# Pairing the scan's k/q loads and the two directions' decay loads in a bidirectional gated DeltaNet layer with windowed attention

## The chip, the cores and the metric

One NeuronCore of one Trainium2 chip runs the whole layer. The metric is the device time of one execution, in microseconds (us). Where a profile is read, one execution of the same program was taken by the hardware profiler; its time and its span are given beside the median of the unprofiled runs.

## What is computed

The layer takes x (2048 tokens of width 1024), normalises it, projects it once, and feeds two head groups: a gated DeltaNet with 4 heads of width 128 that is scanned forward and backward, and windowed attention with 8 query heads. Their outputs are concatenated, projected and added to x. Only the DeltaNet's part bears on the change. For each head and direction, with g the running sum of the log decays inside a chunk:

```python
decay = jnp.exp(jnp.where(incl, g[..., :, None] - g[..., None, :], -jnp.inf))
m = jnp.where(strict, jnp.einsum('bhncd,bhnsd->bhncs', k_beta, k) * decay, 0.0)
a_intra = jnp.where(incl, jnp.einsum('bhncd,bhnsd->bhncs', q, k) * decay, 0.0)
...
def step(state, inp):
    q_i, k_i, u_i, w_i, g_i, a_i = inp
    v_new = u_i - jnp.einsum('bhcd,bhde->bhce', w_i, state)
    o = (jnp.einsum('bhcd,bhde->bhce', q_i * jnp.exp(g_i)[..., None], state)
         + jnp.einsum('bhcs,bhse->bhce', a_i, v_new))
...
    state = state * jnp.exp(g_last)[..., None, None] + jnp.einsum('bhcd,bhce->bhde', k_dec, v_new)
```

All arithmetic is in 32-bit floats. The kernel uses chunks of 128 tokens, so a head has 16 chunks (NCH = 16) and each direction takes 16 dependent steps.

## The kernel before, in words

**Phase A** (`phase_a`) projects x, convolves, and writes intermediates to scratch tensors in device memory (DRAM): k and q of head h transposed into `kq_d[h]` (128 feature rows, a plane for k and one for q, 2048 token columns), v into `v_d[h]`, and the gates. It computes the windowed attention too. In its second half it calls `delta_setup` (L431), which forms the running decay sums and writes them as a small table `gr_d` (L496 to L502): for each direction d, 64 rows of 128 values, row c*4+h for chunk c and head h. The sums of one head over four neighbouring chunks therefore lie in four pieces of 128 values (512 bytes) that are 2 KB apart. For head 0 only (NDEC = 1) `delta_setup` also computes the full decay matrices ahead of time: for each group of four chunks and each direction it loads the table's pieces broadcast to 128 partitions (L512), adds the mask on GpSimd (L513), takes exponentials on ScalarE (L515) and stores the result in `dec_d[0, d]` (L516).

**Phase B** (`phase_b`) runs four heads. `pre_front(h)` (L637) prepares head h in four groups of four chunks: it loads k and q (L654), v (L656) and, for each direction, the decays: for head 0 from `dec_d` (L661), for heads 1 to 3 from `gr_d` by a broadcast load (L664), followed by the mask (L665, GpSimd) and the exponential (L702, ScalarE). The decay tile `gm` has one 256 KB buffer for each direction and group, four in all. The products k·k and q·k (L694, tile `gh`) are scaled by the decays into `ma` (L703, VectorE), and part of `ma` goes to DRAM (L708) for `solve` and `invert`, which compute the triangular inverses.

`scan(h)` (L798) is the recurrence. In step i the forward direction takes chunk i and the backward direction chunk 15-i, one after the other. Each step but the first loads its own chunk's k and q (L809 and L810, tile `kqc`, 128 KB, four buffers for each direction), multiplies both by the state (L812 and L823), and forms the step's output and the new state. Steps of the two directions do not depend on each other.

Scan h is interleaved with `pre_front`, `solve` and `invert` of head h+1, and with units of the attention half of the output projection (`sw_units`, L567: tiles `mxs`, `zcs`, `xrs`, `pcs`). After the last scan comes the rest of the output projection (`out_dn`, tiles `mxd`, `pcd`, `xrd`).

**What sets the order.** Every DMA is issued from SyncE's queue (SP), in order. The order of all five engines' queues is not that of the source: `set_order` (L938) builds the graph of dependencies, gives each instruction a modelled cost, and repeatedly plans forward and backward (L1174); the best of the later plans becomes the queues. In this planner a DMA costs its queue 500 ns whatever its size (L1095), moves for a time that comes from its longest contiguous pieces (`move`, L1127), lands 2400 ns after that (LAG, L931), and 2000 ns later still if it broadcasts (L1129). A tile's buffer is free for its next user when all users of the old tile are done (L1068).

Of the kernel before, what the change touches and what calls it, by code (L numbers as in the profile page):

```python
# [7 lines left out]
F32 = mybir.dt.float32  # L8
F32R = mybir.dt.float32r
AF = mybir.ActivationFunctionType  # L10
ALU = mybir.AluOpType
# [4 lines left out]
P = 128  # L16
# [3 lines left out]
NCH = 16  # L20
# [4 lines left out]
NDEC = 1  # L25
# [42 lines left out]
def phase_a(ctx, wide, tc, t, ident, nw, bd, gp, mix_sw, kq_d, v_d, zdn_d, zsw_d, q_pool):  # L68
# [317 lines left out]
    for half in range(2):  # L386
# [18 lines left out]
        if half:  # L405
            consts = delta_setup(tc, t, ident, bd, gp, ap, bp, pj, q_pool)
# [24 lines left out]
def delta_setup(tc, t, ident, bd, gp, ap, bp, pj, q_pool):  # L431
    nc = tc.nc
    V, A, G, T = nc.vector, nc.scalar, nc.gpsimd, nc.tensor
    dma = nc.sync.dma_start

    def const(name, shape, src=None, pool=gp):
        a = pool.tile(shape, F32, tag=name, name=name)
        if src is not None:
            dma(a, src)
        return a  # L440

    s1 = bp.tile([P, 1030], F32, tag="big", name="su1")
    s2 = bp.tile([P, 1030], F32, tag="big", name="su2")
    tri = s1[:, : 3 * P].rearrange("p (a n) -> p a n", a=3)
    gc = s1[:, 3 * P : 5 * P].rearrange("p (a n) -> p a n", a=4)
    dma(tri, t["tri"])
    dmask = const("dmask", [P, 2, P], t["dmask"])
    dnw = const("dnw", [P, 1], t["dnw"])
    al = const("al", [P, 8], t["al"].partition_broadcast(P), ap)
    dtb = const("dtb", [P, 8], t["dtb"].partition_broadcast(P), ap)  # L450
    pw = const("pw", [P, 2, 16])
    V.memset(pw[:, 0], 0.5)
    V.memset(pw[:, 1], -0.5)
    A.activation(dnw, dnw, AF.Copy, scale=0.5)

    beta = const("beta", [P, NCH, 8])
    A.activation(beta, bd[:, :, 0:8], AF.Tanh, scale=0.5)
    V.tensor_scalar(beta, beta, 0.5, 0.5, ALU.mult, ALU.add)
    u, e, w, m, z0, g = (s2[:, k * P : (k + 1) * P].rearrange("p (c e) -> p c e", e=8) for k in range(6))
    V.tensor_tensor(u, bd[:, :, 8:16], dtb.unsqueeze(1).to_broadcast([P, NCH, 8]), ALU.add)  # L460
    V.tensor_scalar(e, u, -1.0, None, ALU.mult)
    V.tensor_tensor(e, e, u, ALU.min)
    A.activation(al, al, AF.Exp)
    A.activation(e, e, AF.Exp)
    V.tensor_scalar(w, e, 1.0, None, ALU.add)
    A.activation(m, w, AF.Ln)
    V.tensor_scalar(w, w, -1.0, None, ALU.add)
    V.tensor_scalar(z0, w, 0.0, None, ALU.is_equal)
    V.tensor_tensor(m, m, z0, ALU.add)
    V.tensor_tensor(w, w, z0, ALU.add)  # L470
    V.reciprocal(w, w)
    V.tensor_tensor(m, m, w, ALU.mult)
    V.tensor_tensor(m, m, e, ALU.mult)
    V.tensor_scalar(u, u, 0.0, None, ALU.max)
    V.tensor_tensor(u, u, m, ALU.add)
    V.scalar_tensor_tensor(g, u, -1.0, al.unsqueeze(1).to_broadcast([P, NCH, 8]), ALU.mult, ALU.mult)

    gps = pj.tile([P, 512], F32, tag="pj", name="gps")[:, :256].rearrange("p (a n) -> p a n", a=4)
    for d in range(2):
        gv = g[:, :, 4 * d : 4 * d + 4]  # L480
        T.matmul(gps[:, d], tri[:, d], gv, start=True, stop=True)
        T.matmul(gps[:, 2 + d], tri[:, 2], gv, start=True, stop=True)
    V.tensor_copy(gc, gps)
    negc, ngc, egt, ekd, egc = (const(nm, [P, 2, NCH, 4]) for nm in ("negc", "ngc", "egt", "ekd", "egc"))
    gf, tf = gc[:, 0:2], gc[:, 2:4]

    def fl(a):
        return a.rearrange("p d c h -> p d (c h)")

    V.tensor_scalar(fl(ngc), gf, -1.0, None, ALU.mult)  # L490
    V.tensor_tensor(fl(ekd), tf, gf, ALU.subtract)
    A.activation(ekd, ekd, AF.Exp)
    A.activation(fl(egt), tf, AF.Exp)
    A.activation(fl(egc), gf, AF.Exp)
    V.tensor_scalar(negc, egc, -1.0, None, ALU.mult)
    gr_d = q_pool.tile([2, 64, P], F32, tag="gr_d", name="gr_d")  # L496
    for d in range(2):
        gt = pj.tile([P, 512], F32, tag="pj", name=f"gt{d}")[:64, :P]
        T.transpose(gt, gc[:, d], ident)
        gs = s1[:64, (5 + d) * P : (6 + d) * P]  # L500
        V.tensor_copy(gs, gt)
        dma(gr_d[d], gs)  # L502
    dec_d = {}
    for h in range(NDEC):
        for d in range(2):
            dec_d[h, d] = q_pool.tile([4, P, 512], F32, tag=f"dec{h}_{d}", name=f"dec{h}_{d}")
        for c4 in range(4):
            s4 = slice(4 * c4, 4 * c4 + 4)
            for d in range(2):
                gm = ap.tile([P, 4, P], F32, tag="gm", name=f"gm{h}_{c4}_{d}", bufs=2)  # L510
                src = gr_d[d].rearrange("(c h) i -> c h i", h=4)[s4, h]
                dma(gm, src.partition_broadcast(P))  # L512
                G.tensor_tensor(gm, gm, dmask[:, d : d + 1].to_broadcast([P, 4, P]), ALU.add)  # L513
                for c in range(4):
                    A.activation(gm[:, c], gm[:, c], AF.Exp, bias=ngc[:, d, 4 * c4 + c, h : h + 1])  # L515
                dma(dec_d[h, d][c4], gm.rearrange("p c i -> p (c i)"))  # L516
    return dmask, dnw, pw, beta, negc, ngc, egt, ekd, egc, gr_d, dec_d


def phase_b(ctx, wide, late, tc, t, ident, consts, hp, mix_dn, mix_sw, kq_d, v_d, zdn_d, zsw_d, dp, out):  # L520
    nc = tc.nc
    V, A, G, T = nc.vector, nc.scalar, nc.gpsimd, nc.tensor
    dma = nc.sync.dma_start

    def pool(name, bufs=1, stack=ctx, **kw):
        return stack.enter_context(tc.tile_pool(name=name, bufs=bufs, reuse_waits="tile", **kw))

    dmask, dnw, pw, beta, negc, ngc, egt, ekd, egc, gr_d, dec_d = consts
# [88 lines left out]
    q1 = pool("q1", stack=pre_stack)  # L617
# [11 lines left out]
    def ma_tile(h, p):  # L629
        tag = f"ma{FREED[p] if h > 1 else p}"  # L630
        return hd[h % 2].tile([P, 4, 4, P], F32, tag=tag, name=f"ma{h}_{p}", bufs=1)
# [5 lines left out]
    def pre_front(h):  # L637
# [12 lines left out]
        for n, c4 in enumerate(FRONT):  # L650
            s4 = slice(4 * c4, 4 * c4 + 4)
# [2 lines left out]
            dma(kq, kq_d[h][:, :, cs])  # L654
            vt = q1.tile([P, 512], F32, tag="vt", name=f"vt{h}_{c4}", bufs=2)
            dma(vt, v_d[h][:, cs])  # L656
            gms = []
            for d in range(2):
                gm = q1.tile([P, 4, P], F32, tag="gm", name=f"dc{h}_{c4}_{d}", bufs=4)
                if h < NDEC:  # L660
                    dma(gm.rearrange("p c i -> p (c i)"), dec_d[h, d][c4])  # L661
                else:
                    src = gr_d[d].rearrange("(c h) i -> c h i", h=4)[s4, h]
                    dma(gm, src.partition_broadcast(P))  # L664
                    G.tensor_tensor(gm, gm, dmask[:, d : d + 1].to_broadcast([P, 4, P]), ALU.add)  # L665
                gms.append(gm)
                p = 3 - c4 if d else c4
                if p not in mp:
                    mp[p] = ma_tile(h, p)
                ma[d, c4] = mp[p][:, :, 1 - d :: 2]  # L670
            for j, ss in ((0, ssk), (1, ssq)):
# [6 lines left out]
                for c in range(4):  # L678
                    cc = 4 * c4 + c
                    src = ks[c4] if j == 0 else tr  # L680
# [9 lines left out]
            for c2 in range(2):  # L690
                gh = ps_g.tile([P, 2, 2, P], F32, tag="gh", name=f"gh{h}_{c4}_{c2}")
                for k in range(2):
                    c = 2 * c2 + k
# [3 lines left out]
                for k in range(2):  # L697
                    c = 2 * c2 + k
# [99 lines left out]
    def scan(h, H):  # L798
        ks, vs, ck, ma = (H[k] for k in ("ks", "vs", "ck", "ma"))
        oacc = H["oacc"] = {}  # L800
        st = {}
        for i in range(NCH):
            for d in range(2):
                c = i if d == 0 else NCH - 1 - i
                c4, cl = c // 4, c % 4
                sc = slice(c * P, (c + 1) * P)
                nm = f"{h}_{d}_{i}"
                if i:
                    kqc = rp.tile([P, 2, P], F32, tag=f"kqc{d}", name=f"kqc{nm}", bufs=4)  # L809
                    dma(kqc, kq_d[h][:, :, sc])  # L810
                    pk = ps_s.tile([P, P], F32, tag="pk", name=f"pk{nm}")
                    T.matmul(pk, kqc[:, 0], st[d], start=True, stop=True)  # L812
                    r = rp.tile([P, P], F32, tag="r", name=f"r{nm}")
                    V.scalar_tensor_tensor(  # L814
                        r, pk, negc[:, d, c, h : h + 1], vs[c4][:, cl], ALU.mult, ALU.add
                    )
                else:
                    r = vs[c4][:, cl]
# [68 lines left out]
    with tc.using_default_side("right"):  # L887
        zp = pool("zp", 2, stack=wide)
    H = pre_front(0)
    for f in late:  # L890
        f(zp)
# [7 lines left out]
    with tc.using_default_side("right"):  # L899
        rp = pool("rp", 2)  # L900
# [5 lines left out]
    for h in range(3):  # L906
        scan(h, H)
        H = pre_front(h + 1)
        solve(h + 1, H)
        invert(h + 1, H)  # L910
# [8 lines left out]
    def out_dn(c):  # L919
# [3 lines left out]
        out_half(op, lambda j, nm: ps_c.tile([P, 512], F32, tag="pc", name=nm), w, mx, part_d[c], out[sc, :], f"d{c}", 2)  # L923

    scan(3, H)
    for c in ORD:
        out_dn(c)
# [381 lines left out]
```

## Time and profile before

| what | us |
|---|---|
| median of 3 runs | 1280.27 |
| lowest and highest run | 1278.16 and 1280.57 |
| the profiled execution, its own time | 1274.25 |
| the profiled execution, span from first to last instruction | 1272.5 |

The profiled execution's granted TensorE clock had a mean of 0.992. Engines are named PE (TensorE's matmuls), PEld (its weight loads), DVE (VectorE), ACT (ScalarE), POOL (GpSimd), SP (SyncE, which issues DMAs). L810 is line 810 of the kernel. `out<-in` names the tiles that an instruction writes and reads. In tables by stretch of time, each engine has its busy us and the number of instructions; "DMA share" is the mean busy share of the core's 16 DMA engines, and GB/s what they moved. In chronological lists a bracket holds the idle time of that engine just before the instruction, and what ended it.

### The profile page before, as it was taken

Reading aid. Unit: us, or ns where it says so; the run is one execution under the profiler, and the core shown is the slowest. Engines: PE = TensorE matmul, PEld = TensorE weight load, DVE = VectorE, ACT = ScalarE, POOL = GpSimd, SP = SyncE. Lnnn points to the kernel's source line nnn. Section 1 sums busy time; section 2 is a strip of 40 time slices with the busy share of each in tenths; the row PEclk is TensorE's granted clock in tenths of the full one; section 3 lists DMA queues with packets and bytes.
Section 4 is the critical chain, followed back from the end, with each engine's and each line's share of the span. In section 5 each row is a group of like instructions: output and inputs, shape, how many; then the busy total and the mean of one; then the engine's idle time right before and its main releaser. Section 6 shows DMA issues by size and latency. Waiting matters only on the chain.

```text
span 1272.5 us, 22253 instructions
## 1 busy us (share of the span) xinstructions
PE 1219.4 (96%) x7066; PEld 1044.4 (82%) x7066; DVE 889.5 (70%) x2154; ACT 703.2 (55%) x2105; POOL 507.4 (40%) x893
## 2 busy tenths in 40 slices
PE   6999999999999999999999998998799899999998
PEld 6998877788889998787788787887688789798876
DVE  4422387999975589999986573788488879557333
ACT  6321254776644677776654425858557955566210
POOL 1330044666613398665221306613672651641000
PEclk9999999999999999999999998999899999999999
DMA  8442254322544434522137826967965974746675
GB/s 269 145 132 76 95 180 128 97 97 81 180 132 144 130 96 116 158 87 67 58 117 244 224 96 189 276 189 207 270 169 154 269 191 138 217 145 214 227 242 205
DMA packets 225510, 205.34 MB, mean 161 GB/s; under 512 B 48497, under 2 KB 175089, under 8 KB 225393
## 3 DMA queue, kind: packets, MB, share of 16 engines
q1 hardware_dynamic: 225392, 203.92, 52.7%
q8 instruction: 56, 0.92, 0.3%
q14 instruction: 62, 0.50, 0.1%
HBM read 138.79 MB, written 65.08 MB: 160 GB/s over the span
## 4 chain that ended last, share of the span: by engine, by line
PE 67%; DVE 12%; DMA 9%; ACT 7%; issue 3%; POOL 1%; SPq 0%; DVEq 0%; ACTq 0%; POOLq 0%
PE pf_c L191 4%; PE pf_c L192 4%; PE pf_c L193 4%; PE pf_z L191 4%; PE pf_z L192 4%; PE pf_z L193 4%; PE pi L772 4%; DVE acc L242 3%; PE pt L363 3%; PE pq_q L202 2%; PE pq_q L204 2%; PE pq_q L203 2%; PE pcd L561 2%; PE pcd L563 2%; PE pcd L562 2%
## 5 line engine op out<-in xcount | busy, mean ns | idle before, releaser
L191 PE MATMUL pf_c<-xhi,wh_c 128*128 128x512 f32 x384 | 151.0, 404 | 0.7 <-DVE acc L242 0.4
L192 PE MATMUL pf_c<-xlo,wh_c 128*128 128x512 f32 x384 | 150.6, 401 | 0.0
L193 PE MATMUL pf_c<-xhi,wl_c 128*128 128x512 f32 x384 | 149.1, 401 | 0.0
L242 DVE SCALAR_TENSOR_TENSOR acc<-pf_c,cw,acc 128x512 f32<-128x512 f32 (+1 forms) x192 | 140.3, 743 | 11.3 <-ACT acc L238 9.2
L358 POOL TENSOR_SCALAR pr<-pr,st 128x384 f32<-128x384 f32 (+1 forms) x128 | 80.1, 648 | 71.3 <-DVE st L356 60.0
L191 PE MATMUL pf_z<-xhi,wh_z 128*128 128x512 f32 x256 | 86.6, 401 | 0.5 <-DVE zo L215 0.5
L349 ACT ACTIVATE pr<-pr,st 128x384 f32<-128x384 f32 (+1 forms) x128 | 76.1, 596 | 19.6 <-DVE st L345 19.1
L192 PE MATMUL pf_z<-xlo,wh_z 128*128 128x512 f32 x256 | 86.2, 399 | 0.0
L191 PEld LDWEIGHTS pf_c<-xhi,wh_c 128*128 128x128 f32 x384 | 72.1, 188 | 15.3 <-DVE acc L242 1.7
L193 PE MATMUL pf_z<-xhi,wl_z 128*128 128x512 f32 x256 | 84.7, 397 | 0.0
L192 PEld LDWEIGHTS pf_c<-xlo,wh_c 128*128 128x128 f32 x384 | 72.3, 188 | 13.0
L193 PEld LDWEIGHTS pf_c<-xhi,wl_c 128*128 128x128 f32 x384 | 71.8, 188 | 13.0
L345 DVE CUSTOM_DVE_ANT_0 pr<-s,mask,sink 128x384 f32<-128x384 f32 (+1 forms) x128 | 72.5, 593 | 12.4 <-PE s L344 8.3
L367 ACT ACTIVATE ph<-pt 128x512 fp32r<-128x512 f32 x92 | 53.0, 596 | 40.9 <-PE pt L363 39.1
L826 ACT ACTIVATE yk<-py,ck 128x128 f32<-128x128 f32 x120 | 43.9, 366 | 49.5 <-PE py L821 48.4
L363 PE MATMUL pt<-ident,pr 128*128 128x128 f32 x368 | 67.2, 274 | 1.9 <-DVE q L327 1.1
L368 DVE TENSOR_TENSOR pl<-pt,ph 128x512 fp32r<-128x512 f32 x92 | 61.6, 681 | 5.1 <-ACT ph L367 5.0
L703 DVE SCALAR_TENSOR_TENSOR ma<-gh,bp,dc 128x256 f32<-128x256 f32 x128 | 54.9, 476 | 10.4 <-PE gh L694 8.7
L363 PEld LDWEIGHTS pt<-ident,pr 128*128 128x128 f32 x368 | 46.5, 140 | 17.7 <-DVE pl L368 3.0
L202 PE MATMUL pq_q<-wh_q,xhi 128*128 128x256 f32 x256 | 60.3, 285 | 0.6 <-ACT sgkv L261 0.3
L599 PE MATMUL pcs<-wohs,mhs 128*128 128x512 f32 x128 | 57.7, 451 | 2.9 <-ACT mhs L593 2.3
L814 DVE SCALAR_TENSOR_TENSOR r<-pk,negc,vs 128x128 f32<-128x128 f32 x120 | 41.5, 346 | 27.1 <-PE pk L812 26.6
(251 smaller groups left out, 3709.8 us busy)
## 6 DMA issues: line engine op xcount, KB each, us to landing
kqc<-kq_d SPq DMA_DIRECT2D x120, 128.0 KB, 3.0
ws_c<-wt SPq DMA_DIRECT2D x48, 256.0 KB, 3.3
xr<-x SPq DMA_DIRECT2D x16, 512.0 KB, 6.3
ws_z<-wt SPq DMA_DIRECT2D x32, 256.0 KB, 3.9
kq<-kq_d SPq DMA_DIRECT2D x16, 512.0 KB, 5.3
m_d<-ma SPq DMA_DIRECT2D x32, 256.0 KB, 5.4
mxs<-mix_sw SPq DMA_DIRECT2D x32, 256.0 KB, 3.8
xrs<-x SPq DMA_DIRECT2D x32, 256.0 KB, 3.6
```

What stands on the lines that cost most here:

```text
L191: T.matmul(ps, hi[:, k, cs], xhi[b][:, k], start=(k == 0), stop=False)
L192: T.matmul(ps, hi[:, k, cs], xlo[b][:, k], start=False, stop=False)
L193: T.matmul(ps, lo[:, k, cs], xhi[b][:, k], start=False, stop=(k == KC - 1))
L202: T.matmul(ps[:, :n], xh, hi[:, k, :n], start=(k == 0), stop=False)
L242: V.scalar_tensor_tensor(av, ps[:, lo:], cw[:, i, k : k + 1], av, ALU.mult, ALU.add)
L345: V.tensor_tensor_reduce(pr[j][:, :n], ps[:, :n], mask[:, lo * P : hi * P], 1.0, sink[:, hh : hh + 1], ALU.add, ALU.min, accum_out=nm[:, j ...
L349: A.activation(pr[j][:, :n], pr[j][:, :n], AF.Exp, bias=nm[:, j : j + 1], scale=-1.0, accum_out=den[:, j : j + 1])
L358: G.tensor_scalar(pr[j][:, :n], pr[j][:, :n], den[:, j : j + 1], 1.0, ALU.mult, ALU.mult)
L363: T.transpose(pt[:, j], pr[j][:, (kb - lo) * P : (kb - lo + 1) * P], ident)
L368: V.tensor_tensor(pl, ptf, ph.bitcast(F32), ALU.subtract)
L599: T.matmul(ps, mh[:, k], wh[:, k], start=(k == 0), stop=False)
L703: V.scalar_tensor_tensor(ma[d, c4][:, c], gh[:, k], bp[:, d, cc : cc + 1], gms[d][:, c : c + 1].to_broadcast([P, 2, P]), ALU.mult, ALU.mult,)
```

## The change

Three edits go together. The scan's load now brings two consecutive steps of one direction (256 KB in a tile with two buffers instead of four of half the size); the last step, 15, has a load of its own, so a head and direction has 8 loads instead of 15. The decays of both directions of a group come in one load of 512 KB, into one tile with two buffers instead of four of half the size. The tables are laid out anew: `gr_d` by head, then direction, then chunk, so that a head's four chunks are one contiguous piece of 2 KB; `dec_d[0]` with the two directions side by side. The stores into `gr_d` keep pieces of 512 bytes, and `delta_setup` keeps its number of loads and stores. The buffers take the same space as before.

```diff
-    gr_d = q_pool.tile([2, 64, P], F32, tag="gr_d", name="gr_d")
+    gr_d = q_pool.tile([4, 2, NCH, P], F32, tag="gr_d", name="gr_d")
...
-        dma(gr_d[d], gs)
+        dma(gr_d[:, d].rearrange("h c i -> c h i"), gs)
...
-            dec_d[h, d] = q_pool.tile([4, P, 512], F32, tag=f"dec{h}_{d}", name=f"dec{h}_{d}")
+        dec_d[h] = q_pool.tile([4, P, 2, 512], F32, tag=f"dec{h}", name=f"dec{h}")
...
-                src = gr_d[d].rearrange("(c h) i -> c h i", h=4)[s4, h]
-                dma(gm, src.partition_broadcast(P))
+                dma(gm, gr_d[h, d, s4].partition_broadcast(P))
...
-                dma(dec_d[h, d][c4], gm.rearrange("p c i -> p (c i)"))
+                dma(dec_d[h][c4][:, d], gm.rearrange("p c i -> p (c i)"))
...
+            gms = q1.tile([P, 2, 4, P], F32, tag="gm", name=f"dc{h}_{c4}", bufs=2)
+            if h < NDEC:
+                dma(gms.rearrange("p d c i -> p d (c i)"), dec_d[h][c4])
+            else:
+                dma(gms.rearrange("p d c i -> p d (c i)"), gr_d[h][:, s4].rearrange("d c i -> d (c i)").partition_broadcast(P))
+            gms = [gms[:, d] for d in range(2)]
             for d in range(2):
-                gm = q1.tile([P, 4, P], F32, tag="gm", name=f"dc{h}_{c4}_{d}", bufs=4)
-                if h < NDEC:
-                    dma(gm.rearrange("p c i -> p (c i)"), dec_d[h, d][c4])
-                else:
-                    src = gr_d[d].rearrange("(c h) i -> c h i", h=4)[s4, h]
-                    dma(gm, src.partition_broadcast(P))
-                    G.tensor_tensor(gm, gm, dmask[:, d : d + 1].to_broadcast([P, 4, P]), ALU.add)
-                gms.append(gm)
+                if h >= NDEC:
+                    G.tensor_tensor(gms[d], gms[d], dmask[:, d : d + 1].to_broadcast([P, 4, P]), ALU.add)
...
-                    kqc = rp.tile([P, 2, P], F32, tag=f"kqc{d}", name=f"kqc{nm}", bufs=4)
-                    dma(kqc, kq_d[h][:, :, sc])
+                    if i % 2:
+                        two[d] = rp.tile([P, 2, 2 * P], F32, tag=f"kqc{d}", name=f"kqc{nm}", bufs=2)
+                        n = min(2, NCH - i) * P
+                        c0 = c * P - (n - P) * d
+                        dma(two[d][:, :, :n], kq_d[h][:, :, c0 : c0 + n])
+                        low[d] = c0
+                    kqc = two[d][:, :, c * P - low[d] : (c + 1) * P - low[d]]
```

More of the change, by code (lines that the diff above doesn't have):

```diff
@@ L501, in delta_setup @@
         V.tensor_copy(gs, gt)
-        dma(gr_d[d], gs)
+        dma(gr_d[:, d].rearrange("h c i -> c h i"), gs)
     dec_d = {}
     for h in range(NDEC):
-        for d in range(2):
-            dec_d[h, d] = q_pool.tile([4, P, 512], F32, tag=f"dec{h}_{d}", name=f"dec{h}_{d}")
+        dec_d[h] = q_pool.tile([4, P, 2, 512], F32, tag=f"dec{h}", name=f"dec{h}")
         for c4 in range(4):
@@ L656, in pre_front @@
             dma(vt, v_d[h][:, cs])
-            gms = []
-            for d in range(2):
-                gm = q1.tile([P, 4, P], F32, tag="gm", name=f"dc{h}_{c4}_{d}", bufs=4)
-                if h < NDEC:
-                    dma(gm.rearrange("p c i -> p (c i)"), dec_d[h, d][c4])
-                else:
-                    src = gr_d[d].rearrange("(c h) i -> c h i", h=4)[s4, h]
-                    dma(gm, src.partition_broadcast(P))
-                    G.tensor_tensor(gm, gm, dmask[:, d : d + 1].to_broadcast([P, 4, P]), ALU.add)
-                gms.append(gm)
+            gms = q1.tile([P, 2, 4, P], F32, tag="gm", name=f"dc{h}_{c4}", bufs=2)
[4 more added lines that the diff above has]
+            gms = [gms[:, d] for d in range(2)]
+            for d in range(2):
+                if h >= NDEC:
+                    G.tensor_tensor(gms[d], gms[d], dmask[:, d : d + 1].to_broadcast([P, 4, P]), ALU.add)
                 p = 3 - c4 if d else c4
@@ L800, in scan @@
         oacc = H["oacc"] = {}
-        st = {}
+        st, two, low = {}, {}, {}
         for i in range(NCH):
@@ L805, in scan @@
                 c4, cl = c // 4, c % 4
-                sc = slice(c * P, (c + 1) * P)
                 nm = f"{h}_{d}_{i}"
                 if i:
-                    kqc = rp.tile([P, 2, P], F32, tag=f"kqc{d}", name=f"kqc{nm}", bufs=4)
-                    dma(kqc, kq_d[h][:, :, sc])
+                    if i % 2:
[5 more added lines that the diff above has]
+                    kqc = two[d][:, :, c * P - low[d] : (c + 1) * P - low[d]]
                     pk = ps_s.tile([P, P], F32, tag="pk", name=f"pk{nm}")
```

## The prediction

> **What bounds the kernel now.** I read the page first: totals, busy tenths in 40 slices, and the chain that ended last by engine.
>
> ```profile
> span 1272.5 us, 22253 instructions
> PE 1219.4 (96%) x7066; PEld 1044.4 (82%) x7066; DVE 889.5 (70%) x2154; ACT 703.2 (55%) x2105; POOL 507.4 (40%) x893
> ...
> PE   6999999999999999999999998998799899999998
> ...
> DMA  8442254322544434522137826967965974746675
> ...
> PE 67%; DVE 12%; DMA 9%; ACT 7%; issue 3%; POOL 1%; SPq 0%; DVEq 0%; ACTq 0%; POOLq 0%
> ```
>
> PE is the bound: busy 1219.4 of 1272.5 us, so 53.1 us without a matmul is all that a better supply of data could give back. The PE row says where that lies: the first slice, and slices 25 to 30, about 763 to 954 us, with high digits of the DMA row in the same place. The table by stretch resolves it (columns: length, then busy us of PE, PEld, DVE, ACT, POOL, granted clock, DMA share, GB/s).
>
> ```profile
> 550.00:670.00 120.00, 119.18 (x591) 95.85 (x590) 114.12 (x259) 76.86 (x183) 50.56 (x73) 1.00 0.26 83
> 774.00:830.00 56.00, 48.90 (x320) 43.80 (x320) 35.03 (x87) 46.90 (x183) 34.23 (x71) 0.94 0.91 265
> 830.00:870.00 40.00, 39.70 (x276) 35.76 (x276) 36.76 (x114) 23.68 (x90) 7.97 (x11) 1.00 0.62 184
> 870.00:930.00 60.00, 48.45 (x287) 40.61 (x286) 35.62 (x115) 38.24 (x164) 30.88 (x57) 0.91 0.87 244
> 930.00:980.00 50.00, 48.28 (x350) 44.21 (x349) 44.80 (x131) 33.04 (x117) 27.54 (x51) 1.00 0.51 154
> 980.00:1020.00 40.00, 35.27 (x239) 30.41 (x238) 35.23 (x114) 36.24 (x162) 22.91 (x48) 1.00 0.89 249
> 1020.00:1165.00 145.00, 141.20 (x1019) 127.92 (x1017) 98.24 (x298) 86.06 (x304) 60.63 (x141) 1.00 0.61 178
> ```
>
> In three stretches, 774 to 830, 870 to 930 and 980 to 1020, the DMA share is 0.87 to 0.91 and PE is idle for 7.1, 11.6 and 4.7 us: 23.4 us together. These are the times at which the next head's k, q, v and decays are loaded beside the scan. Between them, at shares of 0.51 to 0.62, PE loses 0.3, 1.7 and 3.8 us. The change touches the loads of these stretches and nothing of PE's work, so whatever it brings must come out of the 23.4 us, and the price of a mishap falls into the same stretches.
>
> Next, the views of the two tiles (name, count: shortest, median, longest ns on the issuing queue, first and last start), and from the page the time from issue to landing.
>
> ```profile
> L810 SPq DMA_DIRECT2D kqc<-kq_d x120: 517/530/1568, 774.0 to 1157.1; - x120
> L664 SPq DMA_DIRECT2D dc<-gr_d x24: 383/590/1681, 705.1 to 1003.7; - x24
> L661 SPq DMA_DIRECT2D dc<-dec x8: 326/532/1125, 668.2 to 698.0; - x8
> ```
>
> ```profile
> kqc<-kq_d SPq DMA_DIRECT2D x120, 128.0 KB, 3.0
> kq<-kq_d SPq DMA_DIRECT2D x16, 512.0 KB, 5.3
> dc<-gr_d SPq DMA_DIRECT2D x24, 256.0 KB, 6.1
> ```
>
> **The change part by part.** *Issue on SP.* A head and direction has 8 loads of k and q instead of 15, so 64 instead of 120. At the median of 0.53 us that is 63.6 us before and 33.9 us after, if a load of twice the size costs the queue the same. The nearest row is the load of four chunks of the same tensor, 512 KB, whose issue took 0.56 us; it stands below. So 29.7 us go from a queue that needs them over 383 us (774.0 to 1157.1). The decays' 32 loads in phase B become 16, which saves half of the 24 and half of the 8: 12 × 0.59 + 4 × 0.53 = 9.2 us. SP has no part in the chain's shares (SPq 0%), so none of the 39 us is a gain by itself; it counts only where a later DMA on the queue is waited for by PE. I looked for such a place among PE's waits. One stands out.
>
> ```profile
> 774.01 1.21 SPq L810 DMA_DIRECT2D kqc<-kq_d  x2
> ...
> 777.37 3.49 SPq L810 DMA_DIRECT2D kqc<-kq_d  x5
> ...
> 783.53 0.53 SPq L810 DMA_DIRECT2D kqc<-kq_d  x1
> 784.16 0.56 SPq L654 DMA_DIRECT2D kq<-kq_d  x1
> ...
> 790.38 1.09 PE L674 MATMUL tr<-ident,kq 128*128 128x128 f32 x4 [3.86 <-DMA kq<-kq_d]
> ```
>
> SP issues eight scan loads (1.21 + 3.49 + 0.53 = 5.2 us) just ahead of the load `kq` at 784.16, and PE stands still for 3.86 us until that lands. Four double loads at 0.56 us take 2.2 us, so `kq` can be issued up to 3.0 us earlier. The bytes ahead of it stay the same, though, and the engines that move them are at a share near 0.9 here, so the landing moves by between 0 and 3.0 us. I take the middle, **1.5 us**.
>
> *Time of the transfers.* The same bytes move in longer pieces: k and q in 1 KB instead of 512 bytes, the broadcast decays in 2 KB instead of 512 bytes. No row times a piece by its size, so I bound it by the rate at full share: 244 / 0.87 = 280 GB/s from 870 to 930, where these loads are thick, and 83 / 0.26 = 319 GB/s from 550 to 670, where there are none. All the difference given to piece size is an upper bound, 12%; none is the lower. Heads 1 to 3 each load 2.1 MB of decays and, in the crowded stretch, about half of their 3.9 MB of k and q: 4 MB, 14.3 us at 280 GB/s and 12.5 at 319. So 0 to 1.8 us of transfer a head. PE idles for part of a crowded stretch only, and other waits end there too (below), so I take about half the bound, 1 us a head: **3 us**.
>
> The Trainium skill, "DMA: Bandwidth & Descriptors", section Specifications, has 512 bytes as the smallest transfer at line rate; this would speak against the second term, since the pieces have that size already. By it the sum would be 1.5 us instead of 4.5. The trace's 280 against 319 GB/s allows either, because the first stretch also holds scattered stores of other tiles.
>
> *What is coarser.* The load of a pair can start only when both steps of the pair before last are done. The pace comes from the scan's first matmul, two instructions a step:
>
> ```profile
> L812 PE MATMUL pk<-S,kqc x110: 270/275/377, 1024.9 to 1163.5; 128*128 128x128 f32 x110
> ```
>
> 55 steps in 138.6 us are 2.5 us each, 5 us for a step of both directions. With two double buffers the other pair's two steps, 10 us, lie between the release and the use; a 256 KB load has to land in that time, and the rows give 3.0 us for 128 KB, 5.3 for 512 KB. Five us are left, and I cost it at nothing; if steps come at half that interval the cover is gone. The combined decay load lands later for its first direction by at most the 0.9 us that 256 KB take at 280 GB/s; the mask on POOL (40% busy) waits for it, and behind it ScalarE's exponentials. That is hidden as long as the load is issued a group ahead, as the buffers allow exactly as before; if not, it is up to 0.9 us for each of 12 loads, but against two loads of 6.1 us that now wait behind each other on SP I cost it at zero. The eight broadcast loads of `delta_setup` and its stores keep their count, and run from 470 to 548 us beside a PE that is full there; longer pieces can only shorten them: nothing.
>
> *The order.* All queues are planned anew, since 72 entries of 500 ns go from the planner's SP queue. This can shift any instruction. Its worth is bounded by the rows: above by the 23.4 us of idle PE, below by new gaps like the present ones. I take zero, and keep both sides for the range.
>
> **Sum.** 1.5 + 3 = 4.5 us less. The profiled execution took 1274.25 us, of which 1.75 lie around the span; it would become 1269.8. The median of the runs shown is 6.0 us above it, and I subtract from the median: 1280.3 - 4.5 = **1275.8 us**.
>
> **The rivals.** *The clock comes back too.* After the gap at 786 the granted clock (third from last) is halved for some time:
>
> ```profile
> 788.00:790.00 2.00, 0.00 (x0) 0.00 (x0) 0.00 (x0) 1.26 (x4) 1.75 (x7) 0.61 1.01 290
> 790.00:792.00 2.00, 1.62 (x8) 1.66 (x9) 0.38 (x2) 0.50 (x1) 0.67 (x3) 0.50 0.94 266
> 792.00:794.00 2.00, 2.00 (x11) 2.00 (x11) 2.00 (x5) 1.63 (x10) 0.00 (x0) 0.50 0.94 223
> 794.00:796.00 2.00, 2.00 (x14) 2.00 (x13) 0.40 (x3) 1.03 (x9) 0.00 (x0) 0.69 1.06 320
> ...
> 900.71 1.76 PE L694 MATMUL gh<-kq 128*128 128x256 f32 x4 [2.38 <-DVE ma L703]
> 902.00:904.00 2.00, 1.53 (x6) 0.72 (x4) 1.49 (x4) 1.51 (x6) 1.70 (x2) 0.50 0.84 256
> ```
>
> The losses 0.39, 0.50, 0.50 and 0.31 of 2 us each are 3.4 us of clock. If the shorter gap no longer triggers it, these come on top: 1275.8 - 3.4 = 1272.4. Against it: a gap of 2.38 us was also followed by a clock of 0.50, and 3.86 - 1.5 leaves 2.36. Chance 0.15. The Trainium skill, "TensorE: Matmul & The Clock Gate", Part 1, lets the clock fall only after an idle window of about 3.4 us, which would favour this rival; the gap of 2.38 us speaks against so long a threshold.
>
> *The transfers were hidden anyway.* If piece size does not matter, and the crowded stretches wait for their dependent chains and not for bandwidth, only the first term is left: 1280.3 - 1.5 = 1278.8, no measurable change. For it: from 870 to 930 the longest PE gaps have VectorE as releaser, as in the row at 900.71. Chance 0.17.
>
> *SP waits longer, and what is behind it comes late.* This is the slower one. SP's own waits in phase B are mostly those of the scan's loads:
>
> ```profile
> SPq L810 <- PE po L830: 35.8, 29, 3.5
> SPq L810 <- PE py L821: 26.5, 19, 4.3
> ```
>
> SP stands 62 us in these two rows for a buffer's release by PE, up to 4.3 us at a time, and everything behind on the queue stands too: the next head's `kq`, decays, `mxs`, `xrs`. A pair's load waits for the later of two steps, and the planner places it by modelled times that PE does not keep. From the point at which the release comes later than planned by more than the lead of the transfer queued behind, PE waits for that transfer. One such gap a head, of the 2.4 us seen above, in three heads is 7.2 us: 1280.3 + 7.2 = 1287.5. For it: the plan shifts anyway, and PE has no slack in which to hide a bad place. Against it: about half as many such waits, and 5 us of lead. Chance 0.33. That the change doesn't do what it says can hardly be: the counts are fixed by the loops.
>
> **How the numbers follow.** Forecast 0.35, clock 0.15, hidden 0.17, slower 0.33. Of 1280.3 us, 0.2% (about what a measurement of this kernel can tell from no change) is 2.6 us: faster means below 1277.7, slower above 1282.8. Faster: 0.15 of the clock case, 0.29 of the forecast's 0.35, 0.03 of the hidden case: 0.47. Same: 0.06 of the forecast, 0.12 hidden, 0.03 of the slower case: 0.21. Slower: 0.30 and 0.02 from the hidden case: 0.32. The forecast's own range is 1268.5 (1280.3 less 3.0 + 3.4 + 5.4, both bounds and the clock) to 1280. The whole range goes down to 1266, 2.5 us more for a luckier order, and up to 1290, the slower rival with one gap more: 1266 to 1290.
>
> **What would show it.** In the profile after: 64 loads `kqc` of 256 KB (8 of them 128 KB) at 0.5 to 0.6 us and 16 decay loads of 512 KB; no PE wait named after `kqc`; the gap before the first `tr` matmul of head 1 in the scan shorter than 3.86 us; PE idle in the crowded stretches below 23.4 us in sum at an unchanged matmul count. Wrong would be: issue times of 1 us for the double loads, PE waits on `kqc`, SP waits at L810 that exceed today's, or new gaps elsewhere that the new order brings.

## The result, and the profile after

The changed kernel takes 1282.78 us (median of 20 runs, 1278.74 to 1289.51), the kernel before 1279.24 us (20 runs, 1276.57 to 1286.84). The ratio is 1.003 with a 95% interval of 1.0018 to 1.0043: slower by 0.3%, about 3.5 us. I had forecast 1275.8 us and a gain; 1282.8 us lies in the slower part of the range that I gave (1266 to 1290).

The page of the profile after (span, busy time of each engine, busy tenths):

```profile
span 1276.5 us, 22062 instructions
PE 1217.9 (95%) x7066; PEld 1043.0 (82%) x7066; DVE 889.4 (70%) x2154; ACT 703.4 (55%) x2105; POOL 511.3 (40%) x893
...
PE   6999999999999999999999998999889899998998
```

The work is unchanged, PE's 7066 matmuls too. PE stands idle for 1276.5 - 1217.9 = 58.6 us where it was 53.1, that is 5.5 us more, and its busy time is 1.5 us shorter.

The same table by stretch (length, busy us of PE, PEld, DVE, ACT, POOL, granted clock, DMA share, GB/s):

```profile
550.00:670.00 120.00, 119.52 (x595) 95.77 (x594) 114.85 (x265) 77.71 (x188) 52.36 (x77) 1.00 0.24 81
774.00:830.00 56.00, 48.65 (x310) 42.49 (x309) 30.52 (x85) 44.40 (x172) 40.34 (x90) 0.97 0.91 261
830.00:870.00 40.00, 38.38 (x268) 34.82 (x267) 35.44 (x105) 23.59 (x85) 5.95 (x9) 1.00 0.59 176
870.00:930.00 60.00, 48.81 (x303) 41.12 (x301) 41.66 (x126) 41.02 (x177) 29.43 (x50) 0.94 0.91 249
930.00:980.00 50.00, 47.91 (x345) 43.48 (x344) 42.41 (x122) 30.99 (x107) 32.90 (x59) 1.00 0.50 153
980.00:1020.00 40.00, 34.70 (x221) 28.40 (x220) 33.82 (x114) 35.78 (x166) 14.48 (x18) 1.00 0.82 244
1020.00:1165.00 145.00, 142.32 (x1046) 131.46 (x1045) 102.35 (x307) 88.90 (x311) 68.92 (x170) 1.00 0.59 175
```

The three crowded stretches lose 7.4, 11.2 and 5.3 us, 23.8 together against 23.4 before. So the relief that I had worked out for them is not seen as PE time. The quieter stretches between and behind them lose 1.6, 2.1 and 2.7 us. From 774 to 1165 us, where the changed loads of the scan run, that makes 30.2 us against 29.2: only 1.0 of the 5.5 us. The rest is scattered ahead of this and behind it, and no single place holds the loss.

The changed loads themselves, from the views of the tiles and, for the landing, the page:

```profile
L809 SPq DMA_DIRECT2D kqc<-kq_d x64: 518/530/824, 777.9 to 1165.6; - x64
L659 SPq DMA_DIRECT2D dc<-gr_d x12: 370/457/1202, 709.1 to 1004.5; - x12
L657 SPq DMA_DIRECT2D dc<-dec x4: 371/516/634, 671.5 to 701.2; - x4
```

```profile
kqc<-kq_d SPq DMA_DIRECT2D x56, 256.0 KB, 3.6
...
dc<-gr_d SPq DMA_DIRECT2D x12, 512.0 KB, 7.4
```

A load of twice the size costs SP the same 0.53 us, and it lands 0.6 us later; the double decay load lands 7.4 us after issue, where each single one took 6.1. The DMA queue's row, first of before, then of after (packets, MB, share of 16 engines' span):

```profile
q1 hardware_dynamic: 225392, 203.92, 52.7%
```

```profile
q1 hardware_dynamic: 197104, 203.92, 51.9%
```

0.527 × 1272.5 = 670.6 us of transfer became 0.519 × 1276.5 = 662.5 us: the same bytes in longer pieces took 8.1 us less. The same product over all profiles on record is 663.3 to 670.6 us with the old loads (seven profiles, of seven different orders) and 654.4 to 662.5 us with the new ones (seven), 7.0 us apart on average, so the saving does not hang on this pair. And the gap that I had singled out, in chronological lists of SP and of PE:

```profile
777.87 1.21 SPq L809 DMA_DIRECT2D kqc<-kq_d  x2
...
781.32 0.70 SPq L809 DMA_DIRECT2D kqc<-kq_d  x1
...
782.94 0.61 SPq L809 DMA_DIRECT2D kqc<-kq_d  x1
...
786.95 0.53 SPq L652 DMA_DIRECT2D kq<-kq_d  x1
```

```profile
793.76 1.11 PE L671 MATMUL tr<-ident,kq 128*128 128x128 f32 x4 [2.23 <-DMA kq<-kq_d]
```

Four loads in 2.5 us stand ahead of `kq` instead of eight in 5.2, and PE's gap is 2.23 us instead of 3.86. Yet `kq` and the matmul that needs it do not come earlier in the execution: they start at 786.95 and 793.76 us, and started at 784.16 and 790.38. What changed is the lead: `kq` goes out 4.6 us before PE runs out of work (786.95 to 791.53), where it was 2.4 (784.16 to 786.52). How much of that is the shorter queue and how much the new order can't be read from this pair of profiles. The transfers are shorter, the issues are fewer, and the kernel is not faster; the runs below ask why. The last row to see is SP's waiting in phase B (total, times, longest):

```profile
SPq L809 <- PE po L831: 35.1, 22, 8.8
...
SPq L809 <- PE pcs L597: 14.0, 5, 6.6
```

The queue waits fewer times for a buffer of the scan, but for up to 8.8 us at a time, where the longest was 4.3.

### The profile page after: what moved, and what is told of

Read it like the earlier page. It is cut to its first block, busy times and chain, and to the rows that moved or that the text cites. A ratio compares the mean times of both kernels' runs of the same rounds, so it can differ in the third digit from the quotient of the medians.

```text
span 1276.5 us, 22062 instructions
## 1 busy us (share of the span) xinstructions
PE 1217.9 (95%) x7066; PEld 1043.0 (82%) x7066; DVE 889.4 (70%) x2154; ACT 703.4 (55%) x2105; POOL 511.3 (40%) x893
## 4 chain that ended last, share of the span: by engine, by line
PE 69%; DVE 11%; DMA 10%; ACT 5%; issue 2%; POOL 2%; SPq 1%; DVEq 0%; ACTq 0%; POOLq 0%
PE pf_c L191 5%; PE pf_c L193 5%; PE pf_c L192 5%; PE pf_z L191 4%; PE pf_z L193 4%; PE pf_z L192 4%; PE pi L769 4%; PE pt L363 3%; DVE acc L242 2%; PE pcd L559 2%; PE pcd L561 2%; PE pcd L560 2%; PE pq_q L202 2%; PE pq_q L204 2%; PE py L822 2%
## 5 line engine op out<-in xcount | busy, mean ns | idle before, releaser
L349 ACT ACTIVATE pr<-pr,st 128x384 f32<-128x384 f32 (+1 forms) x128 | 76.0, 596 | 22.5 <-DVE st L345 22.4
L203 PE MATMUL pq_q<-wh_q,xlo 128*128 128x256 f32 x256 | 59.6, 282 | 0.0
```

What stands on the lines that cost most here:

```text
L203: T.matmul(ps[:, :n], xl, hi[:, k, :n], start=False, stop=False)
L349: A.activation(pr[j][:, :n], pr[j][:, :n], AF.Exp, bias=nm[:, j : j + 1], scale=-1.0, accum_out=den[:, j : j + 1])
```

## The experiments

All ratios are to the kernel before, timed beside it on the same chip, with 95% intervals.

**The theories.** A: the new order of the queues costs the 0.3%, not the loads. B: the coarser loads cost it, by later release and later landing. Later came C (any order is worth some tenths of a per cent either way), D (an order is worth what its loads allow) and E (the loads are worth a little in any order planned for them).

**One part alone, all queues planned anew.** The scan's edit alone, then the edits of decays and tables alone, each as in the diff above.

> Only the scan's loads are paired; decays and tables as before; all queues planned anew. Theory B with the pairs as its cause: 1.003, the whole loss. Theory B with the decays as its cause: 1.000. Theory A: no value is foreseen, any new order may come out between 0.996 and 1.006, and its PE idle time need not lie at the loads.

> Only the decays' loads and tables are changed; the scan loads single steps as before; all queues planned anew. Theory B with the decays as its cause: 1.003. Theory B with the pairs as its cause: 1.000. Theory A: no value is foreseen, between 0.996 and 1.006; and the sum of the losses of this run and of the one with the scan alone need not be 0.3%.

Measured: scan alone 0.9951 (0.9932 to 0.997), decays alone 1.0001 (0.9986 to 1.0017). Theory B had the whole loss in one of the two, and neither shows it. The parts do not add up to 1.003, and the paired loads alone are faster than either kernel (1271.66 us). Nor did that gain come from where I had looked for it:

```profile
774.00:830.00 56.00, 46.10 (x298) 40.57 (x297) 32.72 (x85) 44.52 (x175) 35.90 (x76) 0.97 0.94 262
870.00:930.00 60.00, 50.30 (x296) 41.34 (x296) 38.98 (x115) 40.06 (x166) 31.93 (x58) 0.94 0.91 251
980.00:1020.00 40.00, 34.83 (x237) 30.06 (x236) 34.05 (x111) 35.57 (x161) 23.92 (x49) 1.00 0.89 257
```

In this scan-only kernel the crowded stretches cost PE 9.9, 9.7 and 5.2 us, 24.8 in sum, more than before. Its SP waits for a pair's buffer as long as that of the changed kernel does:

```profile
SPq L812 <- PE po L834: 40.8, 16, 8.8
```

So a wait of SP of this length does not by itself make a kernel slow.

**Orders exchanged.** The order of one kernel's queues is recorded and imposed on the other as further edges in the planner. PE, DVE, ACT and POOL have the same instructions in both, one for one.

```diff
+    for e, text in FIXED.items():
+        mine = [k for k in range(n) if insts[k][1] == e]
...
+                started[old].append(mine[at])
```

> The changed kernel's loads and tables, but PE, DVE, ACT and POOL are held to the order that they had in the kernel before, instruction for instruction; only SP's queue is planned anew. Theory A (the new order of the compute engines costs the 0.3%, the loads themselves cost nothing): 0.997 to 1.001 of the kernel before. Theory B (the coarser loads cost it: pairs wait for a later release, the double decays land later): 1.003 again, and PE waits that end at loads.

> The mirror image: the loads and tables of the kernel before, with the four compute engines held to the order that they have in the changed kernel. Theory A: about 1.002 to 1.005 of the kernel before, as slow as the changed kernel. Theory B: 0.999 to 1.001, since the loads are the old ones.

> Control for the run with the changed loads and the old order of the compute engines: the kernel before with its own order held on PE, DVE, ACT and POOL, and SP's queue planned anew. It computes and loads exactly what the kernel before does. If 1.002 to 1.005: a new SP order alone costs what that run lost, and nothing is laid to the loads. If 0.999 to 1.001: the new SP order is harmless, and the 1.004 of that run is the loads'.

Measured: new loads in the old compute order 1.0043 (1.0023 to 1.0062); old loads in the new compute order 1.0019 (1.0001 to 1.0037); the control, old loads and old compute order with only SP planned anew, 0.9985 (0.997 to 0.9999). The old order did not rescue the new loads, so A as I had put it falls: in this compute order the new loads, with the SP queue planned for them, cost 0.4%. The second run shows that the new order costs about 0.2% with the old loads too. SP's queue is planned anew in all three, so none of them shows the loads alone.

**All five queues held to the old order**, SP's too. A pair's load stands where the load of its second step stood, so inside a head it waits for the same step's release as that load did; a double decay load stands where the first of the two was.

> Only the scan's loads paired, all five queues held to the order of the kernel before. My prediction's mechanism (SP and the transfers relieved): 0.996 to 0.999, since 56 issues of 0.53 us go and nothing else changes. Order alone as the cause of the 0.995 of the replanned scan-only kernel: 1.000. Pairs costly by themselves: above 1.002.

> Only the decays' loads and tables changed, all five queues held to the order of the kernel before. If the double decay loads cost something by themselves (the first direction lands later, 512 KB in one go): 1.001 to 1.003, with more waiting of POOL's mask for dc. If not: 0.999 to 1.000.

> The changed kernel's loads and tables with all five queues held to the order of the kernel before, SP's too: each pair's load stands where the load of its second step stood, each double decay load where the first of the two stood. Theory A (order): 0.996 to 1.001. Theory B (the coarser loads themselves): 1.003 to 1.005, with PE waits that end at loads or at ma.

Measured: pairs 1.0173 (1.0155 to 1.0191), decays 1.0057 (1.004 to 1.0075), both 1.0231 (1.0209 to 1.0253). Each part costs by itself here, and the two add up: 1.73 + 0.57 = 2.30%. That is several times what B had foreseen (1.003 to 1.005 for both, 1.001 to 1.003 for the decays). My mechanism (fewer issues, hence faster) is refuted for this unchanged order, with the loads in these places; other places were not tried. The slower rival of my prediction is what happens. In the pairs-only profile PE is idle for 1299.0 - 1225.1 = 73.9 us, 20.8 more than before, and its busy time is 5.7 us longer at a mean granted clock of 0.983 instead of 0.992. SP's waits in the pairs-only kernel:

```profile
SPq L812 <- PE po L834: 36.8, 16, 9.9
...
SPq L812 <- PE po L827: 22.1, 8, 6.3
```

SP stands for up to 9.9 us for the release of a pair. One consequence can be followed through the queues; first SP, then PE, in that kernel:

```profile
1004.48 0.53 SPq L812 DMA_DIRECT2D kqc<-kq_d  x1
1005.10 0.55 SPq L886 DMA_DIRECT2D mix_dn<-zt  x1
1009.49 0.53 SPq L812 DMA_DIRECT2D kqc<-kq_d  x1
...
1011.27 0.53 SPq L654 DMA_DIRECT2D kq<-kq_d  x1
```

```profile
1016.95 1.12 PE L674 MATMUL tr<-ident,kq 128*128 128x128 f32 x4 [4.17 <-DMA kq<-kq_d]
```

Between 1005.65 and 1009.49 SP issues nothing: it waits for the buffer of the next pair. `kq`, the next head's load, stands behind it and goes out at 1011.27, and PE is idle for 4.17 us until it lands. In the kernel before, the same place of the queue reads:

```profile
993.39 0.76 SPq L810 DMA_DIRECT2D kqc<-kq_d  x1
...
995.38 0.53 SPq L810 DMA_DIRECT2D kqc<-kq_d  x1
...
998.17 0.53 SPq L654 DMA_DIRECT2D kq<-kq_d  x1
```

There `kq` follows within 5 us of the load at 993.39, not 7. The waits for `kq` in sum are hardly longer, though (5.7 us against 4.9 before, since the first gap is now 3.14 us and ends at a ScalarE instruction). Most of the new idle time stands under VectorE and ScalarE, and the longest such wait leads back to SP as well:

```profile
1181.27 2.58 SPq L812 DMA_DIRECT2D kqc<-kq_d  x2
...
1183.94 1.81 SPq L596 DMA_DIRECT2D xrs<-x  x1
...
1188.42 0.69 DVE L602 TENSOR_TENSOR xrs<-xrs,pcs 128x512 f32<-128x512 f32 x1 [5.42 <-DMA xrs<-x]
1189.02 0.35 DVE L818 SCALAR_TENSOR_TENSOR r<-pk,negc,vs 128x128 f32<-128x128 f32 x1
...
1189.52 0.77 PE L825 MATMUL py<-r,ma 128*128 128x128 f32 x2 [5.91 <-DVE r L818]
```

SP's last issue before the first row ended at 1176.86. The load `xrs` of the output projection stands behind two pairs; VectorE waits 5.42 us for it, the scan's `r` stands behind that on VectorE, and PE waits 5.91 us for `r`. So a wait that names VectorE can have its origin in the queue of SP. The other long waits were not followed back.

The longest waits of SP in this kernel lie where one scan ends and the next head's first pair is due, as here:

```profile
884.56 0.32 SPq L656 DMA_DIRECT2D vt<-v_d  x1
893.05 0.53 SPq L812 DMA_DIRECT2D kqc<-kq_d  x1
893.67 0.55 SPq L886 DMA_DIRECT2D mix_dn<-zt  x1
894.32 0.38 SPq L664 DMA_DIRECT2D dc<-gr_d  x1
```

From 884.88 to 893.05 nothing goes out, the next head's decays among it. By the code, a head's first load in a direction needed the buffer of step 12 of the head before; as a pair it needs that of steps 13 and 14, since the single load of step 15 has a double buffer to itself. That this sets the length of the wait is argued; no run gave step 15 a buffer of its own. No PE wait in the traces of the changed, the scan-only and the held kernels names `kqc` itself: the pairs arrive in time, and what stands behind them does not. A decay load needs two releases too: the four single buffers held two groups of both directions, and the double load waits until both directions of the group before last are done. In the decays-only kernel POOL's mask waits 24.3 us for `dc`, where it was 10.8:

```profile
  POOL dc L663: 24.3, 6
```

How this reaches PE was not followed. In that profile PE is idle for 58.1 us instead of 53.1, and its busy time is 1230.6 us instead of 1219.4 at a mean clock of 0.981 instead of 0.992, so most of this part's loss is seen as a lower clock.

**The order alone.** The planner's constants are moved by 1 to 4% and nothing else:

```diff
-            return 500
+            return 490        # or 510
...
-LAG = {"PE": 205, "DVE": 140, "Activation": 160, "Pool": 120, "SP": 2400}
+LAG = {"PE": 205, "DVE": 140, "Activation": 160, "Pool": 120, "SP": 2375}    # or 2450
```

> The kernel before with one constant of its planner moved by 2%: a DMA costs SP's queue 490 ns instead of 500. Loads and work are those of the kernel before; only the order can change. Theory C (any new order is worth some tenths of a per cent up or down, by no rule that the change sets): between 0.995 and 1.006, not 1.000. Theory D (an order is worth what its loads allow): 0.999 to 1.001.

> The kernel before with 510 ns instead of 500 for a DMA in the planner. Theory C: between 0.995 and 1.006 and off the value of the run with 490 by some tenths of a per cent. Theory D: 0.999 to 1.001.

> The changed kernel with 490 ns instead of 500 for a DMA in the planner. Theory C: between 0.995 and 1.007, perhaps faster than the kernel before. Theory D: 1.003, as the changed kernel itself.

> The changed kernel with 510 ns instead of 500 for a DMA in the planner. Theory C: between 0.995 and 1.007, and off the run with 490 by some tenths of a per cent. Theory D: 1.003.

> The kernel before with another constant of the planner moved by 1%: a DMA lands 2375 ns after its transfer instead of 2400. Theory C (order alone, no rule): 0.995 to 1.010. It makes a pair with the changed kernel at the same constant: theory B (the coarser loads cost some 0.3% in any order) wants the changed one 0.3% slower than this one; theory E (the loads are worth a little in any order that is planned for them) wants it 0.2% faster.

> The changed kernel with 2375 ns instead of 2400 in the planner. Theory B: 0.3% above the kernel before at the same constant. Theory E: 0.2% below it. Theory C: either sign, some tenths of a per cent.

> The kernel before with 2450 ns instead of 2400 in the planner. Theory C: 0.995 to 1.010. The pair with the changed kernel at 2450: theory B 0.3% slower, theory E 0.2% faster.

> The changed kernel with 2450 ns instead of 2400 in the planner. Theory B: 0.3% above the kernel before at the same constant. Theory E: 0.2% below it. Theory C: either sign.

> Only the scan's loads paired, with 490 ns instead of 500 for a DMA in the planner; the fast scan-only kernel (0.995) at another order. If the pairs themselves brought the gain: 0.993 to 0.998 again, and below the kernel before at 490 ns (1.0034) by 0.5%. If its order did: anywhere between 0.997 and 1.010.

> Only the scan's loads paired, with 510 ns instead of 500 in the planner. If the pairs themselves brought the gain: below the kernel before at 510 ns (1.0101) by 0.5%, about 1.005. If its order did: anywhere between 0.997 and 1.012.

Measured, with the half-width of the intervals at 0.0013 to 0.0030:

| planner's constants (issue, landing) | before | after | scan's pairs alone |
|---|---|---|---|
| 500, 2400 (as given) | 1 | 1.0030 | 0.9951 |
| 490, 2400 | 1.0034 | 0.9981 | 1.0037 |
| 510, 2400 | 1.0101 | 1.0104 | 1.0074 |
| 500, 2375 | 1.0055 | 1.0081 | not run |
| 500, 2450 | 1.0052 | 0.9998 | not run |

With the loads of the kernel before, a constant that has nothing to do with the chip moves the time by 0.3 to 1.0%, always up: the order before is the best of its five. D falls with this. C holds in kind, but both kernels at 510 lie above the range that it gave (up to 1.006 and 1.007). Much of what these orders cost lies where the change has nothing: before 774 us, ahead of the first load of the scan, PE is idle for 17.9 us in the kernel before and for 22.6, 26.2, 23.9 and 22.5 us in the four redrawn orders of the same loads (rows 490 to 2450); in the pairs-only kernel above, held to the old order, it is 18.1.

Read across, the change is worth +0.30, -0.53, +0.03, +0.26 and -0.54%. The mean is -0.10% with a standard error of 0.19%. The constant +0.3% of B and the constant -0.2% of E are both contradicted by single rows; a mean effect of some tenths either way stays open. The pairs alone give -0.49, +0.03 and -0.27%, a mean of -0.24% with a standard error of 0.15%: suggestive, not shown.

What in the 0.9951 kernel's order makes it fast isn't settled: PE is idle there for 1269.6 - 1215.0 = 54.6 us, about as long as before, and I found no wait that is gone. What differs is PE's busy time for the same matmuls, 1215.0 us instead of 1219.4, and the mean granted clock, 0.995 instead of 0.992 in the profiles and 0.9947 instead of 0.9901 over all runs of this comparison (6 and 29). The gain is seen as a higher clock; what in the order keeps it up stays open.

## Why the prediction was wrong, point by point

**Right: the counts and the cost of issue.** 64 loads instead of 120 and 16 instead of 32, at 0.53 and 0.46 to 0.52 us.

**Right in part, and in size by luck: the first gap.** I took 1.5 us off the 3.86, the middle between 0 and 3.0; 1.63 went, but in a new order. With the order held and the pairs alone, `kq` goes out 4.0 us before PE runs out of work (783.88 to 787.90) instead of 2.4, which is the mechanism that I meant; the gap there is 0.7 us shorter, and what ends it is ScalarE and no longer `kq`.

**Right as transfers, wrong as time: the longer pieces.** I had bounded the gain by 12% of the changed bytes' transfer. The queue as a whole moved its bytes in 8.1 us less. I then carried about half of the crowded stretches' share over to PE as 3 us. None of it is seen there: 23.4 us of idle PE became 23.8. In these stretches the DMA engines are busy for 0.82 to 0.91 of the time, and a high share alone was no sign that PE waits for bandwidth.

**The step that failed: the order, "I take zero".** I had written that all queues are planned anew and that this can shift any instruction, kept both signs for the range, and then priced it at nothing in the sum, with the loads' gain as the signal. At unchanged loads the order's worth spreads over 1.0% in five tries, against an effect of the loads of a few tenths at most. So the order was large enough to decide the sign of the sum. The right price was not zero either: the four new orders of the kernel before are all slower than its own, by 0.3 to 1.0%, so there a redrawn order costs about 0.6% on average (0.34, 1.01, 0.55, 0.52). Which part of this order makes up the 0.3% of the changed kernel stays open.

**Wrong: "what is coarser" at nothing.** I checked whether a pair lands before it is used (it does, no PE wait names it) and not what stands behind it on SP. In the old order that costs 1.7%, and the decays 0.6%. Planned anew, most of it is avoided. That the planner does this by moving other loads ahead of the waiting one is argued, not shown; SP still waits up to 8.8 us at once.

**The rivals.** The slower one named the right mechanism (SP waits longer, what is behind comes late) and bounded it at 7 us; with the order held it is 22 us for the pairs (1301.64 against 1279.51), and in the changed kernel itself its share can't be told from the order's. "Hidden anyway" fits the transfers: their saving is not seen in PE's idle time. "The clock comes back" had its premise wrong and half of its time right: after the shorter gap the clock falls still, for about half as long (columns as in the table by stretch):

```profile
792.00:794.00 2.00, 0.23 (x1) 0.24 (x2) 0.94 (x2) 1.95 (x4) 1.54 (x3) 0.84 1.09 388
794.00:796.00 2.00, 2.00 (x11) 2.00 (x11) 1.70 (x4) 1.09 (x4) 0.00 (x0) 0.50 1.07 348
796.00:798.00 2.00, 2.00 (x16) 2.00 (x16) 0.17 (x1) 1.98 (x13) 0.43 (x1) 0.81 1.08 344
```

That is 0.32 + 1.00 + 0.38 = 1.7 us of clock, where 3.4 were lost. Over the span the mean clock is 0.996 instead of 0.992; the longer idle time outweighs it. The Trainium skill, "TensorE: Matmul & The Clock Gate", Part 1, asks for an idle window of about 3.4 us; here 2.23 us without a matmul, after a stretch only half busy (1.13 of 2 us from 790 to 792), were enough.

## What to carry to other kernels

Where a planner writes the order of all queues, an edit of the loads is two edits, and the second, a redrawn order, can be the larger: here 1.0% between orders at the same loads. Measure it before trusting a small gain or loss, by moving a constant of the planner on both sides and reading the pairs. And when loads are merged, look past whether the merged load arrives in time: on a queue that issues in order, as SP's here, it waits for the last of its releases, and what it delays is whatever stands behind it.

## What the runs showed that I had not expected

The double broadcast load of 512 KB took SP less time to issue (median 0.457 us) than each single one of 256 KB (0.590, and about 0.50 in most profiles of other orders). The 20 runs of the changed kernel tend to follow the granted clock: the fastest, 1278.74 us, had a mean of 0.996, the slowest, 1289.51 us, one of 0.987; one profile each of two kernels that differ by 0.3% can't rank them.
